# First norm of a diffusion backbone: its two modulation vectors on four column groups of TensorE, and the condition's silu later

## The chip, the cores and the metric

The kernel runs on one core of one Trainium2 chip. The metric is the device time of one execution in microseconds; lower is better. The kernel before took 3016.6 us (median of three runs, 3004.18 to 3018.82).

## The reference, cut to what matters

The network has two layers and works on 640 tokens: 512 latent tokens with a condition vector c and 128 context tokens with a learned vector c_ctx. Each layer is an FFN, a mixer and a second FFN, and each of these is preceded by a modulated norm. What the change touches is the first of them:

```python
mod = jax.nn.silu(cond) @ W['w_mod'][i] + W['b_mod'][i]
m = jnp.split(mod[:, None, :], N_MOD, axis=-1)
h = rms_norm(x, g_pre) * (1 + m[1]) + m[0]
f = (silu(h @ w1) * (h @ w3)) @ w2
x = x + 0.5 * m[2] * rms_norm(f, g_post)
```

Each layer has nine modulation vectors m[0] to m[8] of 1024 numbers for each of the two conditions. A vector is a product of 2 x 1024 by 1024 x 1024 in fp32.

## The kernel before

Tokens stand in columns and the 1024 features in eight tiles of 128 partitions. The tokens are split in two halves, of 384 and 256 columns. The order of instructions on each engine is made by a scheduler from the order of the text, from tile buffers and from its own estimates; it may bring an instruction forward whose inputs and buffers are free. Each engine, and each queue of loads (SP's for weights, ScalarE's for constants and the condition), works through its own order strictly.

The beginning (mods_first, lines 116 to 151). The condition is loaded transposed (1024 x 2, line 120), its silu taken on that small form, and silu_cond (line 124) loads the condition once more, spread over all partitions (1024 KB), and takes the silu of that on ScalarE and VectorE (lines 97 to 101). 24 products of ones run first on TensorE (line 127). Then, for k from 0 to 7, weights come as fp32 blocks of 128 x 1024. The scale m[1] is made on TensorE, in two products per k (line 134): the 128 x 2 condition is the stationary operand, 512 weight columns stream, and a 2 x 512 row builds up in PSUM over k. Of the shift m[0] the second half is made in the same way, one product per k. The first half of m[0] is made on VectorE (mods, lines 103 to 114, called at k < 4): the weight block comes transposed, and a multiply-and-sum over 1024 columns gives 128 numbers of one condition, twice per block. After k = 1 the input x is loaded. After k = 4 the text has x_rstd: squares on ScalarE (L209), sums on VectorE (L213), a small product (L176), a few VectorE steps, a diagonal dg (L190), and a product with ones (L192) that spreads the factor over all partitions. At the end the rows go from PSUM to SBUF on ScalarE (L145), are transposed in pieces of 128 columns (L148), and the bias is added (L149).

Then the norm itself (prenorm): x times the factor on VectorE (L255), scale and shift on GpSimd (L262) or ScalarE (L264), and a split in a high and a low part (L273, L274).

The first FFN. Its first stage has 22 hidden blocks and two token halves, 44 steps: blocks 0 to 2 of the first half, blocks 0 to 2 of the second, and from block 3 on both halves of each block in turn. A step has 48 products (L305 to L307) into two PSUM banks and ends in a tanh on ScalarE (L332) and two VectorE products (L333, L334). Weights of a block come as two raw tiles of 512 KB from SP's queue and are split on ScalarE (L299) and VectorE (L300). There are four raw tiles, shared by the FFN's weights and the modulation weights, and six buffers each for high and low parts; silu_cond takes its scratch tile from the low parts' ring. In run_ffn, after every fourth step (q = 3, 7, ...), mods makes the next modulation vector on VectorE: eight loads and 16 multiply-and-sum instructions (L111). In the first FFN seven vectors are made so, in the second nine; there the condition's buffer has been used by others in between, so silu_cond is called again, after step 10 (argument wait).

Of the kernel before, what the change touches and what calls it, by code (L numbers as in the profile page):

```python
# [9 lines left out]
F32 = mybir.dt.float32  # L10
# [4 lines left out]
ALU = mybir.AluOpType  # L15
PSUM = bass.MemoryType.PSUM

P = 128
# [20 lines left out]
class Net:  # L39
# [76 lines left out]
    def mods_first(self):  # L116

        nc, t = self.nc, self.t
        ct = self.fp.tile([P, KD, 2], F32, name="cond_t")
        nc.sync.dma_start(ct, t["cond_t"])  # L120
        th = self.fp.tile([P, KD, 2], F32, name="cond_s")
        nc.scalar.activation(th, ct, AF.Tanh, scale=0.5)
        nc.vector.scalar_tensor_tensor(ct, th, 1.0, ct, op0=ALU.add, op1=ALU.mult)
        self.silu_cond()
        rows = [[self.psum() for _ in range(2)] for _ in range(2)]
        for _ in range(24):
            nc.tensor.matmul(rows[0][0][:, 0:P], self.ones, self.ones, start=True, stop=True)
        for k in range(KD):
            for i in (1, 0):
                w = self.wp.tile([P, 1024], F32, tag="wl" if i else "wh", name=self.name("w"), bufs=self.nw)  # L130
                c0 = 0 if i else 512
                nc.sync.dma_start(w[:, c0:], t["w_mod_first"][i, k][:, c0:])
                for hf in range(1 - i, 2):
                    nc.tensor.matmul(rows[i][hf][0:2], ct[:, k], w[:, hf * 512:hf * 512 + 512], start=k == 0, stop=k == KD - 1)
            if k == 1:
                for j in range(KD):
                    nc.sync.dma_start(self.x[j], t["x"][:, j, :])
            if k < 4:
                self.mods(0, 0, (k,))
            if k == 4:  # L140
                rs = [self.x_rstd(hf) for hf in range(2)]
        for i in (1, 0):
            r = self.wp.tile([P, 1024], F32, tag="wl", name=self.name("row"), bufs=self.nw)[0:2]
            for hf in range(1 - i, 2):
                nc.scalar.activation(r[:, hf * 512:hf * 512 + 512], rows[i][hf][0:2], AF.Copy, scale=0.5)  # L145
            p, e0 = rows[i][1], 0 if i else 4
            for e in range(e0, KD):
                nc.tensor.transpose(p[:, 2 * e:2 * e + 2], r[:, e * P:(e + 1) * P], self.ident[0:2, 0:2])  # L148
            nc.vector.tensor_tensor(self.mall[:, i, e0:], p[:, 2 * e0:16].rearrange("p (e c) -> p e c", c=2),  # L149
                                    self.bmod[:, 0, i, e0:, None].to_broadcast([P, KD - e0, 2]), op=ALU.add)  # L150
        return [self.mall[:, i] for i in range(2)], rs

    def premod_scale(self, layer, sub, scale):
# [1123 lines left out]
def network(ctx, tc, t, outs):  # L1277
# [38 lines left out]
    with ExitStack() as c:  # L1316
        open_ffn(c)
        M[0][0:2], r = n.mods_first()
        gs, sh = gs_sh(0, 0)
        hs = [n.prenorm(hf, gs, sh, r=r[hf]) for hf in range(2)]  # L1320
        rk.consts()
        rk.dense_open(dram)
        hold = {}

        def after(hf, bank):
            a, b = HALF[hf]
            if hf == 0:
                hold["gs"] = gs_sh(0, 1)
            n.prenorm_to(hf, *hold["gs"], rk.dest, bank)
            for k in range(KD):  # L1330
                nc.sync.dma_start(xd[:, k, a:b], n.x[k][:, a:b])
            rk.shift(hf)
            if hf == 0:
                hold["first"] = rk.stream(1, 0, tag=0)

        run_ffn(0, hs, [(0, j) for j in range(2, 9)], 0, 0, after)
        rk.dense(hold["first"])
    with ExitStack() as c:
        sp = c.enter_context(tc.tile_pool(name="scan", bufs=1))
# [162 lines left out]
```

## Time and profile before

| | |
|---|---|
| median of three runs | 3016.6 us |
| the profiled execution's own time | 3012.7 us |
| its span, first to last instruction | 3010.9 us |
| mean granted clock of TensorE | 0.948 |
| TensorE busy | 2840.5 us, 94% |
| VectorE busy | 1804.1 us, 60% |
| ScalarE busy | 1070.7 us, 36% |
| GpSimd busy | 428.6 us, 14% |
| bytes moved | 384.63 MB, mean 128 GB/s |

The span runs from the first to the last instruction; the execution's own time is 1.8 us longer. PE is TensorE, DVE is VectorE, ACT is ScalarE, POOL is GpSimd; SPq and ACTq are the queues of loads of SyncE and ScalarE. A granted clock of 1.00 is 2.4 GHz, 0.50 is 1.2 GHz. An fp32 product shows as two passes, so 24 products are 48 rows. In brackets behind a row stands how long its engine was idle before it and what ended that.

### The profile page before, as it was taken

The numbers are of one execution on the slowest core, as the hardware profiler recorded it, in microseconds if no ns is written. First come the engines' busy times: TensorE is split into PE (matmuls) and PEld (weight loads), VectorE is DVE, ScalarE is ACT, GpSimd is POOL, SyncE is SP. The second block draws the span as 40 slices with busy tenths as digits, with TensorE's granted clock in tenths as the row PEclk, the third lists the DMA queues.
The fourth block names the chain that finished last, engine by engine and source line by source line (L and its number), as shares of the span: only waits on it lengthen the run. The fifth ranks groups of instructions, "written<-read, shape, count | busy, mean of one in ns | idle before, by whom it ended". The sixth has DMA issues, their size and how long they took to land.

```text
span 3010.9 us, 52286 instructions
## 1 busy us (share of the span) xinstructions
PE 2840.5 (94%) x20970; PEld 2539.9 (84%) x20970; DVE 1804.1 (60%) x3698; ACT 1070.7 (36%) x1916; POOL 428.6 (14%) x510
## 2 busy tenths in 40 slices
PE   8999999898899999999699999999999987999997
PEld 5999998585566666667599999999999986999997
DVE  7996328835566777664869993762332668323336
ACT  3112234234444554553431123541223445222233
POOL 2000033111001111101100004310002431000034
PEclk9999999998878998888899999999999998999999
DMA  6665233435433333124236664422223431222233
GB/s 248 206 221 179 81 126 138 162 119 164 125 91 110 119 120 114 50 66 160 88 127 216 225 220 152 140 93 77 71 81 109 139 124 67 99 71 78 91 119 126
DMA packets 167348, 384.63 MB, mean 128 GB/s; under 512 B 22721, under 2 KB 87873, under 8 KB 166849
## 3 DMA queue, kind: packets, MB, share of 16 engines
q1 hardware_dynamic: 165088, 378.22, 37.3%
q8 instruction: 164, 2.69, 0.4%
q10 hardware_dynamic: 2016, 3.07, 0.3%
q14 instruction: 80, 0.65, 0.1%
HBM read 353.24 MB, written 27.98 MB: 127 GB/s over the span
## 4 chain that ended last, share of the span: by engine, by line
PE 66%; DVE 17%; issue 6%; ACT 5%; DMA 4%; POOL 1%; SPq 0%; DVEq 0%; ACTq 0%; POOLq 0%
PE ps L306 15%; PE ps L305 15%; PE ps L307 15%; DVE cj L111 7%; PE px L699 4%; PE pg L843 2%; DVE wl L300 2%; PE pa L771 1%; DMA raw<-in_w_mod 1%; PE pc L981 1%; DVE t L213 1%; ACT gg L929 1%; PE ps L514 1%; PE px L667 1%; DMA mid<-xs 1%
## 5 line engine op out<-in xcount | busy, mean ns | idle before, releaser
L305 PE MATMUL ps<-hp,wh 128*128 128x384 f32 (+3 forms) x2968 | 920.8, 312 | 16.5 <-ACT hp L273 12.6
L306 PE MATMUL ps<-hp,wh 128*128 128x384 f32 (+3 forms) x2968 | 919.4, 310 | 4.5 <-DVE hp L495 2.1
L307 PE MATMUL ps<-hp,wl 128*128 128x384 f32 (+3 forms) x2968 | 915.9, 309 | 2.2 <-DVE wl L300 2.2
L300 DVE TENSOR_TENSOR wl<-raw,wh 128x1024 fp32r<-128x1024 f32 (+1 forms) x408 | 455.0, 1122 | 466.3 <-ACT wh L299 465.5
L299 ACT ACTIVATE wh<-raw 128x1024 fp32r<-128x1024 f32 (+1 forms) x408 | 388.9, 964 | 795.5 <-PE ps L306 675.2
L305 PEld LDWEIGHTS ps<-hp,wh 128*128 128x128 f32 x2968 | 561.1, 190 | 21.9 <-ACT hp L273 16.0
L306 PEld LDWEIGHTS ps<-hp,wh 128*128 128x128 f32 x2968 | 562.5, 190 | 7.4 <-DVE hp L495 2.3
L307 PEld LDWEIGHTS ps<-hp,wl 128*128 128x128 f32 x2968 | 560.5, 189 | 4.1 <-DVE wl L300 3.8
L359 POOL TENSOR_TENSOR gl<-t,gh 128x384 fp32r<-128x384 f32 (+1 forms) x176 | 237.1, 1348 | 1589.7 <-ACT gh L358 1559.7
L307 PE MATMUL ps<-gh,wl 128*128 128x384 f32 (+1 forms) x1408 | 438.6, 312 | 4.1 <-DVE wl L300 4.1
L306 PE MATMUL ps<-gl,wh 128*128 128x384 f32 (+1 forms) x1408 | 437.0, 311 | 3.8 <-POOL gl L359 3.8
L305 PE MATMUL ps<-gh,wh 128*128 128x384 f32 (+1 forms) x1408 | 437.0, 311 | 2.0 <-ACT gh L358 1.3
L111 DVE CUSTOM_DVE_ANT_0 cj<-raw,cj,bmod 128x1024 bf16<-128x1024 f32 x264 | 339.8, 1287 | 8.0 <-DMA raw<-in_w_mod 3.9
L306 PEld LDWEIGHTS ps<-gl,wh 128*128 128x128 f32 x1408 | 269.2, 191 | 5.5 <-POOL gl L359 4.8
L307 PEld LDWEIGHTS ps<-gh,wl 128*128 128x128 f32 x1408 | 269.4, 192 | 5.2 <-DVE wl L300 4.3
L305 PEld LDWEIGHTS ps<-gh,wh 128*128 128x128 f32 x1408 | 269.2, 191 | 4.0 <-ACT gh L358 1.5
L332 ACT ACTIVATE t<-ps 128x384 f32<-128x384 f32 (+1 forms) x176 | 75.7, 430 | 415.4 <-PE ps L307 415.4
L699 PE MATMUL px<-mid,pw 128*128 128x320 f32 x448 | 179.7, 514 | 7.8 <-DMA mid<-xs 5.5
L334 DVE TENSOR_TENSOR t<-t,ps 128x384 f32<-128x384 f32 (+1 forms) x176 | 85.4, 485 | 160.6 <-PE ps L307 160.3
L333 DVE SCALAR_TENSOR_TENSOR t<-t,ps 128x384 f32<-128x384 f32 (+1 forms) x176 | 85.1, 483 | 121.8 <-ACT t L332 121.8
L699 PEld LDWEIGHTS px<-mid,pw 128*128 128x128 f32 x448 | 82.1, 212 | 43.4 <-issue 14.5
L358 ACT ACTIVATE gh<-t 128x384 fp32r<-128x384 f32 (+1 forms) x176 | 79.9, 456 | 53.7 <-PE ps L307 28.8
(369 smaller groups left out, 3299.9 us busy)
## 6 DMA issues: line engine op xcount, KB each, us to landing
raw<-in_w SPq DMA_DIRECT2D x352, 512.0 KB, 3.2
raw<-in_w_mod SPq DMA_DIRECT2D x132, 512.0 KB, 4.1
mid<-xs SPq DMA_DIRECT2D x224, 160.0 KB, 2.3
pw<-in_w_rkv SPq DMA_DIRECT2D x28, 256.0 KB, 3.2
d<-po SPq DMA_DIRECT2D x28, 160.0 KB, 2.3
w<-in_w_mod_first SPq DMA_DIRECT2D x8, 512.0 KB, 7.7
raw<-in_w_rkv SPq DMA_DIRECT2D x8, 512.0 KB, 4.9
xs<-t SPq DMA_DIRECT2D x16, 191.0 KB, 1.9
```

Of the source, the lines that this page charges most:

```text
L111: nc.vector.tensor_tensor_reduce(self.junk, w, self.cond[:, i], 0.5, self.bmod[:, layer, idx, k:k + 1], ALU.mult, ALU.add, out[:, k, i:i + 1])
L299: nc.scalar.activation(h[:, c], w[:, c], AF.Copy)
L300: (eng or nc.vector).tensor_tensor(l[:, c], w[:, c], h[:, c], op=ALU.subtract)
L305: nc.tensor.matmul(out, wh, xh, start=start, stop=False)
L306: nc.tensor.matmul(out, wh, xl, start=False, stop=False)
L307: nc.tensor.matmul(out, wl, xh, start=False, stop=stop)
L332: nc.scalar.activation(gt, o[0], AF.Tanh, scale=0.5)
L333: nc.vector.scalar_tensor_tensor(gt, gt, 1.0, o[0], op0=ALU.add, op1=ALU.mult)
L334: nc.vector.tensor_tensor(gt, gt, o[1], op=ALU.mult)
L358: nc.scalar.activation(gh, g, AF.Copy)
L359: nc.gpsimd.tensor_tensor(gl, g, gh, op=ALU.subtract)
L699: nc.tensor.matmul(p[:, 0:320], w[k // 4][:, k % 4 * P:k % 4 * P + P], x, start=k == 0, stop=k == KD - 1)
```

## The change

All of m[0] and m[1] of the first norm are made on TensorE. For each k both weight blocks are loaded whole (2 x 512 KB), and four products follow, each 2 x 512, into four PSUM banks, where output c stands on partitions 32c and 32c + 1: each product uses another group of 32 columns of the array. The VectorE products of k < 4 and their loads are gone. The rows are copied out by ScalarE and VectorE, two each; 16 transposes of two rows follow, and four additions of the bias. silu_cond is no longer called in the beginning; the first FFN gets wait = 5: silu_cond is called after step 5, and the modulation vectors are made from step 7 on instead of step 3.

```diff
--- before.py
+++ after.py
@@ -121,33 +121,37 @@
         th = self.fp.tile([P, KD, 2], F32, name="cond_s")
         nc.scalar.activation(th, ct, AF.Tanh, scale=0.5)
         nc.vector.scalar_tensor_tensor(ct, th, 1.0, ct, op0=ALU.add, op1=ALU.mult)
-        self.silu_cond()
-        rows = [[self.psum() for _ in range(2)] for _ in range(2)]
+        rows = [self.psum() for _ in range(4)]
         for _ in range(24):
-            nc.tensor.matmul(rows[0][0][:, 0:P], self.ones, self.ones, start=True, stop=True)
+            nc.tensor.matmul(rows[0][:, 0:P], self.ones, self.ones, start=True, stop=True)
         for k in range(KD):
-            for i in (1, 0):
+            ws = []
+            for i in range(2):
                 w = self.wp.tile([P, 1024], F32, tag="wl" if i else "wh", name=self.name("w"), bufs=self.nw)
-                c0 = 0 if i else 512
-                nc.sync.dma_start(w[:, c0:], t["w_mod_first"][i, k][:, c0:])
-                for hf in range(1 - i, 2):
-                    nc.tensor.matmul(rows[i][hf][0:2], ct[:, k], w[:, hf * 512:hf * 512 + 512], start=k == 0, stop=k == KD - 1)
+                nc.sync.dma_start(w, t["w_mod_first"][i, k])
+                ws += [w[:, 0:512], w[:, 512:1024]]
+            for c in range(4):
+                nc.tensor.matmul(rows[c][32 * c:32 * c + 2], ct[:, k], ws[c], start=k == 0, stop=k == KD - 1)
             if k == 1:
                 for j in range(KD):
                     nc.sync.dma_start(self.x[j], t["x"][:, j, :])
-            if k < 4:
-                self.mods(0, 0, (k,))
             if k == 4:
                 rs = [self.x_rstd(hf) for hf in range(2)]
-        for i in (1, 0):
-            r = self.wp.tile([P, 1024], F32, tag="wl", name=self.name("row"), bufs=self.nw)[0:2]
-            for hf in range(1 - i, 2):
-                nc.scalar.activation(r[:, hf * 512:hf * 512 + 512], rows[i][hf][0:2], AF.Copy, scale=0.5)
-            p, e0 = rows[i][1], 0 if i else 4
-            for e in range(e0, KD):
-                nc.tensor.transpose(p[:, 2 * e:2 * e + 2], r[:, e * P:(e + 1) * P], self.ident[0:2, 0:2])
-            nc.vector.tensor_tensor(self.mall[:, i, e0:], p[:, 2 * e0:16].rearrange("p (e c) -> p e c", c=2),
-                                    self.bmod[:, 0, i, e0:, None].to_broadcast([P, KD - e0, 2]), op=ALU.add)
+        r = self.wp.tile([P, 1024], F32, tag="wl", name=self.name("row"), bufs=self.nw)
+        rw = [r[32 * c:32 * c + 2, 0:512] for c in range(4)]
+        for c in range(4):
+            if c % 2:
+                nc.scalar.activation(rw[c], rows[c][32 * c:32 * c + 2], AF.Copy, scale=0.5)
+            else:
+                nc.vector.tensor_scalar(rw[c], rows[c][32 * c:32 * c + 2], 0.5, None, op0=ALU.mult)
+        for e in range(4):
+            for c in range(4):
+                one = self.ident[32 * c:32 * c + 2, 32 * c:32 * c + 2]
+                nc.tensor.transpose(rows[c][:, 2 * e:2 * e + 2], rw[c][:, e * P:(e + 1) * P], one)
+        for c in range(4):
+            e = slice(c % 2 * 4, c % 2 * 4 + 4)
+            nc.vector.tensor_tensor(self.mall[:, c // 2, e], rows[c][:, 0:8].rearrange("p (e c) -> p e c", c=2),
+                                    self.bmod[:, 0, c // 2, e, None].to_broadcast([P, 4, 2]), op=ALU.add)
         return [self.mall[:, i] for i in range(2)], rs
 
     def premod_scale(self, layer, sub, scale):
@@ -1333,7 +1337,7 @@
             if hf == 0:
                 hold["first"] = rk.stream(1, 0, tag=0)
 
-        run_ffn(0, hs, [(0, j) for j in range(2, 9)], 0, 0, after)
+        run_ffn(0, hs, [(0, j) for j in range(2, 9)], 0, 0, after, 5)
         rk.dense(hold["first"])
     with ExitStack() as c:
         sp = c.enter_context(tc.tile_pool(name="scan", bufs=1))
```

## Rows read from the trace of the kernel before

**Rows 1.** The page: busy time of TensorE, and the chain by engine.
```profile
PE 2840.5 (94%) x20970; PEld 2539.9 (84%) x20970; DVE 1804.1 (60%) x3698; ACT 1070.7 (36%) x1916; POOL 428.6 (14%) x510
...
PE 66%; DVE 17%; issue 6%; ACT 5%; DMA 4%; POOL 1%; SPq 0%; DVEq 0%; ACTq 0%; POOLq 0%
```

**Rows 2.** Windows: stretch, length; busy of PE, PEld, DVE, ACT, POOL; clock; DMA share; GB/s.
```profile
15.00:20.00 5.00, 3.57 (x5) 0.59 (x6) 5.00 (x10) 3.88 (x12) 0.00 (x0) 0.50 1.04 403
...
40.00:45.00 5.00, 4.71 (x11) 0.77 (x9) 2.30 (x7) 1.97 (x4) 0.00 (x0) 1.00 0.01 2
...
50.00:55.00 5.00, 4.75 (x15) 4.76 (x16) 4.20 (x9) 4.86 (x11) 5.00 (x4) 0.50 0.41 140
```

**Rows 3.** Timeline, end of the beginning: start, us, engine, line, what, count [idle before].
```profile
37.91 0.70 PE L192 MATMUL ps<-dg,ones 128*128 128x256 f32 x2 [0.91 <-DVE dg L190]
...
38.54 6.17 PE L134 MATMUL ps<-w,cond_t 128*2 128x512 f32 x14
...
44.47 1.05 ACT L145 ACTIVATE row<-ps 2x512 f32<-2x512 f32 x2
...
45.09 0.90 PE L148 MATMUL ps<-ident,row 2*128 2x2 f32 x12 [0.38 <-ACT row L145]
...
46.45 16.26 POOL L262 TENSOR_SCALAR t<-t,gall,mall 128x384 f32<-128x384 f32 x16 [46.01 <-DVE gall L158]
...
50.25 1.33 PE L305 MATMUL ps<-hp,wh 128*128 128x384 f32 x3 [4.26 <-ACT hp L273]
```

**Rows 4.** By line, VectorE: ns min/median/max, first and last start.
```profile
L111 DVE CUSTOM_DVE_ANT_0 cj<-raw,cj,bmod x8: 1275/1277/1280, 15.6 to 34.0; 128x1024 bf16<-128x1024 f32 x8
...
L101 DVE SCALAR_TENSOR_TENSOR cj<-th,cj x4: 1217/1221/1225, 13.3 to 1548.4; 128x1024 f32<-128x1024 f32 x4
```

**Rows 5.** First FFN: ScalarE's timeline, TensorE's waits (60 to 200 us), SP's queue.
```profile
99.57 0.49 ACT L332 ACTIVATE t<-ps 128x384 f32<-128x384 f32 x1 [6.60 <-PE ps L307]
...
111.61 1.06 ACT L299 ACTIVATE wh<-raw 128x1024 fp32r<-128x1024 f32 x1 [4.67 <-DMA raw<-in_w]
...
276.17 0.49 ACT L332 ACTIVATE t<-ps 128x384 f32<-128x384 f32 x1 [3.24 <-PE ps L307]
...
PE ps L305 <- ACT wh L299: 3.4, 1, 3.4
...
108.38 7.54 SPq L294 DMA_DIRECT2D raw<-in_w  x4
```

**Rows 6.** Second FFN: timelines of ScalarE, its queue, and VectorE.
```profile
1406.90 0.33 ACTq L97 DMA_DIRECT2D cj<-in_cond  x1
...
1544.26 0.38 ACT L332 ACTIVATE t<-ps 128x256 f32<-128x256 f32 x1 [6.55 <-PE ps L307]
1544.54 1.05 ACT L100 ACTIVATE th<-cj 128x1024 f32<-128x1024 f32 x1
...
1551.27 0.49 ACT L332 ACTIVATE t<-ps 128x384 f32<-128x384 f32 x1 [3.32 <-PE ps L307]
...
1789.84 0.49 ACT L332 ACTIVATE t<-ps 128x384 f32<-128x384 f32 x1 [6.63 <-PE ps L307]
...
1548.43 1.22 DVE L101 SCALAR_TENSOR_TENSOR cj<-th,cj 128x1024 f32<-128x1024 f32 x1
```

**Rows 7.** Windows, first FFN: columns as in rows 2.
```profile
80.00:90.00 10.00, 10.00 (x88) 10.00 (x87) 9.89 (x17) 1.89 (x4) 1.43 (x1) 1.00 0.54 179
```

**Rows 8.** DMA issues to 60 us, then from 28 to 29: KB, us to landing.
```profile
w<-in_w_mod_first SPq DMA_DIRECT2D x8, 512.0 KB, 7.7
...
cj<-in_cond ACTq DMA_DIRECT2D x1, 1024.0 KB, 8.4
...
w<-in_w_mod_first SPq DMA_DIRECT2D x1, 256.0 KB, 7.8
```

**Rows 9.** Timeline of TensorE in the scan.
```profile
1411.45 0.22 PE L1011 MATMUL po<-gg,uv 128*64 128x64 f32 x1
1411.45 0.45 PE L1013 MATMUL po<-gg,uv 128*64 128x64 f32 x8
```

## The prediction

> **What bounds the kernel now.** I read the page's busy shares and its chain first. TensorE is busy 94% of the span and is named by 66% of the chain [rows 1], so time that is won before the first FFN product is kept only as long as TensorE finds its weights ready afterwards. The edit touches two stretches: the first 50 us, and the first FFN's first stage, where the other modulation vectors are made on VectorE.
>
> The beginning, by windows: from 15 to 20 us the DMA engines move 403 GB/s with a busy share of 1.04, and VectorE is busy all 5 us; by 40 us the transfers are over [rows 2]. What ends last is then read from the timeline. The second half's rstd product (L192) stands at 37.91 us and has waited for VectorE's dg; only behind it, in TensorE's own order, run the last 14 passes of the modulation products, from 38.54 to 44.71 us, on weights that are already there. ScalarE copies rows out to 45.52, the transposes end at 45.99, GpSimd starts the first normalised tile at 46.45 and TensorE the first FFN product at 50.25 us [rows 3]. So the beginning is held by VectorE: eight products of 1.28 us on the first vector (10.2 us) and two of 1.22 us for the silu [rows 4] lie between the sums of squares and dg.
>
> The FFN, by the tanh of each step, which marks the middle of a step on TensorE: the 24 steps between 99.57 and 276.17 us (12 hidden blocks of two halves) took 176.6 us. In the second FFN 34 steps between 1551.27 and 1789.84 us took 238.6 us, 14.03 us for a block of two halves [rows 5, 6]. At that pace the first FFN's 12 blocks would take 168.4 us, so it loses 8.2 us while VectorE makes modulation vectors (9.89 of 10 us busy [rows 7]). The largest single wait is 3.4 us for a weight split, because the weight's load was issued only at 108.38 us, behind eight modulation loads in SP's queue [rows 5].
>
> **The change, part by part.** (1) *Taken from VectorE*: 10.2 us for good, and 2.4 us of silu to a later place. The rstd of both halves is then made as soon as x has come, and L192 no longer holds the modulation products.
>
> (2) *Loads*. SP issued 8 x 512 + 8 x 256 KB of first-norm weights and 4 x 512 KB for the VectorE part, 8192 KB; it now issues 16 x 512 KB, the same bytes. The condition's 1024 KB is on ScalarE's queue. The last weights were issued just after 28 us and landed 7.8 us later, at about 35.9 us [rows 8]. If the condition's load really moves away, that becomes 1024 KB / 403 GB/s = 2.6 us earlier, 33.3 us. But in the second FFN the same load was issued at 1406.90 us, 138 us ahead of the tanh that needs it [rows 6]: the order puts a load where its buffer is free, not where the text stands. I take 35.9 us, and keep 33.3 for the range.
>
> (3) *Products*. 32 instead of 24 matmuls, of two passes each, 0.43 us a pass ((6.17 - 0.59) / 13 for the 14 in [rows 3]). One after another, four would take 3.44 us for each k, more than the 2.6 us in which their 1 MB comes in; fully side by side, 0.86 us. Four long streams on four column groups stand nowhere in the trace. The nearest rows are the scan's products on two groups of 64 columns: the second pass of one starts at 1411.45 us together with the first of the next, and eight passes take 0.45 us where each lasts 0.22 [rows 9]. Their starts are thus (0.45 - 0.22) / 7 = 0.033 us apart, against 0.053 for 64 columns streamed alone at the pace above (0.43 x 64 / 512). That is 1.6 times the serial pace, as if each matmul's second pass ran beside the next one's first. So I take 5 slots, 2.15 us, for each k: below the 2.6 us of the loads. TensorE keeps up, and after the last weight only its own two matmuls are left, three slots or 1.3 us.
>
> The Trainium skill, "TensorEngine Tiling (Array Packing)", Theoretical Speedup, gives up to 4 times for at most 32 columns; by that the four would take 0.86 us, the end would come 0.4 us sooner and the sum below would be 10.4 us. The scan's pairs, at 1.6 times, don't bear it out for a matmul of two passes.
>
> Products end at 35.9 + 0.2 + 1.3 = 37.4 us, against 44.7.
>
> (4) *Behind the products*. Two copies on each of ScalarE and VectorE, the last of them 0.6 us after the last product (two took 1.05 [rows 3]); 16 transposes of 0.075 us (12 took 0.90 [rows 3]) 1.2 us; four short additions and the scale, where two additions and the scale took 0.46 us from 45.99 to 46.45, 0.9 us; five handovers, estimated at 0.1 us. Sum 3.2 us, where 1.75 us stood before. GpSimd then starts at 40.6 us and the first FFN product comes 3.8 us later as now, at 44.4 us: 5.9 us earlier. With the load of the condition out of the way it is 8.5. If the groups ran one after another, products would fall behind the loads by 0.84 us for each of six k, 5 us, and only about 1 us would be left.
>
> (5) *The silu inside the FFN*. Its tanh needs a buffer of the ring that holds the low weight parts, so it waits for TensorE to finish with block 0: the first half of step 3. With S the start of the FFN that is S + 2.5 us (five us at a granted clock of 0.50, that is 1.2 GHz, as at 50 to 55 us [rows 2]) + three steps of the first half + half a step of the second. A block's 14 us, shared out by columns (384 and 256, an estimate), are 8.4 and 5.6, so that is S + 2.5 + 25.2 + 2.8 = S + 30.5. From the first tanh to the end of the last product took 5.1 us in the second FFN [rows 6], hence S + 35.6. ScalarE is held meanwhile, with the tanh of later steps behind it; eight PSUM banks, two a step, cover that. If the cover were gone it would cost up to those 5.1 us.
>
> (6) *Modulation vectors four steps later*. Each of the seven sets is now loaded between neighbouring weight blocks 4 to 16 (before: 3, 4, 6 ... 14). The weight of block 4 is queued on SP behind eight modulation loads, of which the fifth product pair must end: 10 x 1.28 = 12.8 us, plus two of 1.2 us for the split of block 3 and an estimated 3 us for the steps' own products. That gives S + 53.8. From its issue to ScalarE's split such a load took 111.61 - 108.38 = 3.2 us, the split 1.1 [rows 5], and VectorE's half of it should take the 1.2 us of a product of that size [rows 4]: S + 59.3. Block 4 is needed at S + 2.5 + 56 = S + 58.5. So it is just late; I put 1.5 us of wait there, where 0 and 5 are the ends. Later sets lose about what they lose now without that first wait. Of 8.2 us I expect 4 to be lost: 4 us gained, with -5 and +8 as ends.
>
> **Sum.** 5.9 + 4 = 10 us less. The profiled execution took 3012.7 us (span 3010.9), 3.9 us under the median of the three runs, so 3002.7 on its own footing and 3006.6 on the median's; I say 3006. Half a per cent, 15 us, is about what a measurement of this kernel can tell from no change, so this is a change in the right direction that mostly can't be told from none.
>
> **Rivals.** *More is won.* After its silu the second FFN makes nine vectors and loses almost nothing: 14.03 us a block [rows 6]. If the first FFN now does the same, all 8 us come back, and with the condition's load late the front gives 8.5. That is 16.5 us: 3000. For it: the same mechanism in the same kernel, with TensorE at 10 of 10 us. Against it: there the splits of two more blocks had been done before the first set.
>
> *The groups don't run side by side.* Then the edit doesn't do what it says, TensorE's products set the pace, the front gives 1 us and the FFN 4: 3011. Against it stand the scan's pairs; for it, that those streams are eight times shorter.
>
> *Slower: the silu comes too late.* If its tanh starts only where the text puts it, after step 5 at S + 2.5 + 42 = S + 44.5, everything in (6) comes 14 us later: block 4 is ready at S + 73.3, TensorE waits 14.8 us instead of 1.5, and after such a wait it starts at 1.2 GHz again, 2.5 us more. 10 - 15.8 is 6 us slower than before: 3022. The sign turns once that tanh starts later than about S + 39. Against it: in the second FFN the tanh started 0.28 us after that of a step's middle (1544.26), as its buffer came free [rows 6].
>
> **How the numbers follow.** Forecast 0.55, more won 0.25, serial groups 0.12, slower 0.08. The forecast's own range is 2998 to 3014, from the ends of (2) and (6); with the neighbours and the runs' own spread of 15 us, 2994 to 3019 holds eight times in ten. Faster by over 0.5%: over half of the second case (its time lies just beyond the bound) and a quarter of the first, 0.27. Slower by over 0.5%: a third of the last case, 0.03. Within: 0.70.
>
> **What would show it.** The first FFN product near 44 us (42 to 45); no row of VectorE's modulation product before it; L134 with 64 passes whose starts, in a group of eight, are spread over about 2 us; the last weight landing near 36 us. The tanh of the silu at S + 30; TensorE's wait for a weight split around S + 58 of under 5 us; the middle of step 30 (276.17 before) near 266. It would be wrong if the passes stand 0.43 us apart throughout, if the FFN starts before 41 us, or if TensorE waits over 10 us behind the silu.

## The result, and the profile after

The new kernel took 2993.58 us (median of 9 runs, 2989.17 to 3002.74), the kernel before 3018.95 us in the runs beside it (9 runs, 3004.18 to 3034.62). The ratio is 0.9917 [0.9898, 0.9937]: 25 us less, where 10 were forecast. The profiled execution took 2997.18 us, its span 2995.4. On the page TensorE's busy time is what it was [rows 1], over a shorter span, and its share of the chain rose from 66 to 75%:

```profile
PE 2836.9 (95%) x20990; PEld 2539.7 (85%) x20990; DVE 1796.1 (60%) x3686; ACT 1071.0 (36%) x1915; POOL 423.3 (14%) x510
...
PE 75%; DVE 12%; ACT 4%; issue 4%; DMA 3%; POOL 1%; SPq 0%; DVEq 0%; ACTq 0%; POOLq 0%
```

**The beginning.** Lines after L151 stand four further down than before (the norm's GpSimd row is L266, the FFN's products L309 to L311). The timeline of the new kernel, against [rows 3]:

```profile
3.24 0.39 ACTq L97 DMA_DIRECT2D cj<-in_cond  x1
...
35.60 0.28 PE L150 MATMUL ps<-ident,row 2*128 2x2 f32 x2 [0.71 <-ACT row L144]
...
35.81 1.03 PE L134 MATMUL ps<-w,cond_t 128*2 128x512 f32 x4
...
37.56 0.46 PE L150 MATMUL ps<-ident,row 2*128 2x2 f32 x8 [0.37 <-ACT row L144]
...
38.61 13.17 POOL L266 TENSOR_SCALAR t<-t,gall,mall 128x384 f32<-128x384 f32 x16 [38.17 <-DVE gall L162]
...
41.33 0.69 PE L309 MATMUL ps<-hp,wh 128*128 128x384 f32 x1 [3.31 <-ACT hp L277]
```

Read it from the bottom: the first FFN product stands at 41.33 us instead of 50.25, 8.9 us earlier. GpSimd starts at 38.61, 7.8 us earlier, and the last product of the first vectors ends at 36.84 (35.81 + 1.03) instead of 44.71. The top row shows the condition's 1024 KB still loaded at 3.24 us, although the text calls silu_cond only inside the FFN, after step 5: its buffer was free. Two transposes at 35.60 run ahead of the last four passes, since two rows were finished by then; six more follow right behind those passes (36.77 us).

**The first stage of the first FFN.** In the windows (columns as in [rows 2]) TensorE is full from 60 us on. In the first 20 us of the stage it is not: there it waits for the second half's norm tiles, while GpSimd is still busy with them.

```profile
40.00:50.00 10.00, 8.14 (x32) 7.10 (x33) 6.12 (x12) 7.82 (x18) 10.00 (x13) 0.72 0.15 52
50.00:60.00 10.00, 8.91 (x51) 7.89 (x51) 8.18 (x12) 8.41 (x13) 1.78 (x4) 1.00 0.41 116
60.00:70.00 10.00, 10.00 (x60) 10.00 (x59) 7.51 (x10) 3.33 (x6) 1.56 (x2) 1.00 0.45 161
```

The waits of TensorE, from 30 to 400 us of the new kernel (waiting for; us in total, times, longest) hold no row for the high weight part any more:

```profile
PE ps L309 <- ACT hp L277: 4.0, 4, 3.3
PE ps L150 <- ACT row L144: 1.1, 2, 0.7
PE ps L310 <- DVE hp L278: 0.6, 2, 0.3
PE ps L311 <- DVE wl L304: 0.3, 1, 0.3
```

In the kernel before, from 60 to 400 us, the high part cost 3.8 us (3.4 of them in one wait [rows 5]) and the low part 2.2:

```profile
PE ps L305 <- ACT wh L299: 3.8, 2, 3.4
PE ps L307 <- DVE wl L300: 2.2, 5, 0.5
```

The silu on ScalarE's timeline: the second tanh there is that of block 0's *second* half (256 columns), and behind it, with one weight split between, comes the silu's first instruction, at 58.95 us, 17.6 us after the start of the FFN. The last row is the tanh of the stage's last step on the first half, which stood at 359.97 us before.

```profile
53.52 0.49 ACT L336 ACTIVATE t<-ps 128x384 f32<-128x384 f32 x1
56.75 0.37 ACT L336 ACTIVATE t<-ps 128x256 f32<-128x256 f32 x1
58.95 1.05 ACT L100 ACTIVATE th<-cj 128x1024 f32<-128x1024 f32 x1
62.38 1.05 ACT L100 ACTIVATE th<-cj 128x1024 f32<-128x1024 f32 x1
...
344.92 0.49 ACT L336 ACTIVATE t<-ps 128x384 f32<-128x384 f32 x1 [3.24 <-PE ps L311]
```

On TensorE the second half's first 24 products of block 0 stand right behind the first half's first 24, ahead of everything else of the first half. The next two rows are the first of these products and the first product behind them:

```profile
47.73 0.28 PE L309 MATMUL ps<-hp,wh 128*128 128x256 f32 x1
...
53.78 0.34 PE L309 MATMUL ps<-hp,wh 128*128 128x384 f32 x1
```

They took 6.05 us, since they had to wait for the second half's norm. Without gaps they would take 2.8: half of a step of the second half, whose share of the 14.03 us of a block [rows 6] is 5.6 by columns, an estimate.

The first GpSimd row of the FFN's second stage is the milestone used from here on. First the kernel before, then the new one:

```profile
375.31 1.64 POOL L359 TENSOR_TENSOR gl<-t,gh 128x384 fp32r<-128x384 f32 x1 [290.88 <-ACT gh L358]
```

```profile
360.26 1.64 POOL L363 TENSOR_TENSOR gl<-t,gh 128x384 fp32r<-128x384 f32 x1 [280.07 <-ACT gh L362]
```

So 15.05 us are won by the end of the stage: 8.9 in front of it, and 6.1 in the stage itself, which went from 325.1 us (375.31 - 50.25) to 318.9 (360.26 - 41.33).

### The profile page after: what moved, and what is told of

The parts are those of the page before. It is cut to its first block, busy times and chain, and to the rows that moved or that the text cites. A ratio compares the mean times of both kernels' runs of the same rounds, so it can differ in the third digit from the quotient of the medians.

```text
span 2995.4 us, 52305 instructions
## 1 busy us (share of the span) xinstructions
PE 2836.9 (95%) x20990; PEld 2539.7 (85%) x20990; DVE 1796.1 (60%) x3686; ACT 1071.0 (36%) x1915; POOL 423.3 (14%) x510
## 4 chain that ended last, share of the span: by engine, by line
PE 75%; DVE 12%; ACT 4%; issue 4%; DMA 3%; POOL 1%; SPq 0%; DVEq 0%; ACTq 0%; POOLq 0%
PE ps L310 17%; PE ps L309 17%; PE ps L311 17%; PE px L703 5%; DVE cj L111 4%; PE pg L847 2%; PE pa L775 2%; PE pc L985 1%; DVE wl L304 1%; PE px L671 1%; PE ps L518 1%; ACT gg L933 1%; DVE t L217 1%; PE pc L974 1%; PE pc L993 1%
## 5 line engine op out<-in xcount | busy, mean ns | idle before, releaser
L309 PE MATMUL ps<-hp,wh 128*128 128x384 f32 (+3 forms) x2968 | 920.2, 312 | 12.3 <-ACT hp L277 12.3
L311 PE MATMUL ps<-hp,wl 128*128 128x384 f32 (+3 forms) x2968 | 915.4, 309 | 0.3 <-DVE wl L304 0.3
L309 PEld LDWEIGHTS ps<-hp,wh 128*128 128x128 f32 x2968 | 560.6, 189 | 17.2 <-ACT hp L277 15.8
L311 PEld LDWEIGHTS ps<-hp,wl 128*128 128x128 f32 x2968 | 560.2, 189 | 0.7 <-DVE wl L304 0.5
L311 PE MATMUL ps<-gh,wl 128*128 128x384 f32 (+1 forms) x1408 | 436.9, 311 | 4.1 <-DVE wl L304 4.1
L309 PE MATMUL ps<-gh,wh 128*128 128x384 f32 (+1 forms) x1408 | 435.1, 310 | 2.0 <-ACT gh L362 1.3
L111 DVE CUSTOM_DVE_ANT_0 cj<-raw,cj,bmod 128x1024 bf16<-128x1024 f32 x256 | 329.6, 1288 | 8.3 <-DMA raw<-in_w_mod 3.9
L311 PEld LDWEIGHTS ps<-gh,wl 128*128 128x128 f32 x1408 | 267.8, 190 | 5.2 <-DVE wl L304 4.3
L309 PEld LDWEIGHTS ps<-gh,wh 128*128 128x128 f32 x1408 | 267.5, 190 | 3.8 <-ACT gh L362 1.7
```

The lines of the kernel that those rows point to most:

```text
L111: nc.vector.tensor_tensor_reduce(self.junk, w, self.cond[:, i], 0.5, self.bmod[:, layer, idx, k:k + 1], ALU.mult, ALU.add, out[:, k, i:i + 1])
L309: nc.tensor.matmul(out, wh, xh, start=start, stop=False)
L311: nc.tensor.matmul(out, wl, xh, start=False, stop=stop)
```

## The experiments

The theory after this reading: two gains that need each other. The products on TensorE give some 9 us in front of the FFN; the vectors made four steps later give the stage back its lost time. The first rival: the front alone does it. The second: the silu's new place does it. A third question was whether the column groups really run side by side.

All results in one table. "Start" is the first FFN product, "stage 2" the milestone above, "stage" their difference, "waits" what TensorE waited for weight splits between 60 and 400 us; all in us. A ratio is to the kernel before in the same runs.

| kernel | median | ratio [95%] | start | stage 2 | stage | waits |
|---|---|---|---|---|---|---|
| before | 3018.95 | 1 | 50.25 | 375.31 | 325.1 | 6.0 |
| new | 2993.58 | 0.9917 [0.9898, 0.9937] | 41.33 | 360.26 | 318.9 | 0 |
| products_only | 3013.48 | 0.9984 [0.9961, 1.0007] | 41.76 | 375.10 | 333.3 | 10.4 |
| late_vectors_early_silu | 2995.13 | 0.9928 [0.9902, 0.9954] | 41.94 | 360.86 | 318.9 | 0 |
| before_late_vectors | 3001.22 | 0.9958 [0.9936, 0.9979] | 50.02 | 365.63 | 315.6 | 0 |
| one_group | 3013.96 | 0.9994 [0.9976, 1.0012] | 52.96 | 380.07 | 327.1 | 7.6 |
| half_vectors | 3004.20 | 0.9952 [0.9932, 0.9972] | 49.45 | 365.23 | 315.8 | 0.3 |
| front_without_vector_engine | 3013.62 | one run | 47.95 | 380.53 | 332.6 | 11.5 |
| condition_on_sp | 2991.30 | 0.9910 [0.9883, 0.9938] | 39.99 | 358.94 | 319.0 | 0 |
| vectors_from_11 | 2997.26 | 0.9927 [0.9899, 0.9955] | 41.96 | 361.37 | 319.4 | 0 |
| condition_on_sp_vector_norm | 3009.98 | 0.9973 [0.9952, 0.9995] | 37.81 | 374.55 | 336.7 | 6.5 |

### The two parts, each alone

*products_only*: the new beginning, with the silu and the vectors where they were before.

```diff
+        self.silu_cond()
         rows = [self.psum() for _ in range(4)]
...
-        run_ffn(0, hs, [(0, j) for j in range(2, 9)], 0, 0, after, 5)
+        run_ffn(0, hs, [(0, j) for j in range(2, 9)], 0, 0, after)
```

> The new kernel with the condition's silu back in the beginning and the modulation vectors from step 3 on, as before: only the first norm's products are on the four groups. If the beginning and the first FFN's first stage gain separately, the first FFN product starts near 41.5 to 43 us (41.3 in the new kernel, 50.25 before), the stage still loses some 8 us to late weight splits, and the whole gains 9 us against before (ratio 0.997). If the later vectors are worth nothing and all the gain is from the beginning, it gains as much as the new kernel, 25 us (ratio 0.992).

Measured: 0.9984 [0.9961, 1.0007]. The FFN starts 8.5 us earlier than before, and stage 2 at 375.10, 0.2 us earlier. The whole gain in front was handed back inside the stage; the waits of TensorE from 60 to 400 us tell at which point:

```profile
PE ps L310 <- ACT wh L304: 7.1, 4, 4.3
PE ps L312 <- DVE wl L305: 3.3, 3, 1.6
```

*late_vectors_early_silu*: the new kernel with the silu back in the beginning, the vectors still from step 7.

```diff
+        self.silu_cond()
         rows = [self.psum() for _ in range(4)]
...
-            if q == wait and wait:
+            if q == wait and wait and i:
                 n.silu_cond()
```

> The new kernel with the silu back in the beginning, but the vectors still from step 7 on. If it is the later start of the vectors that removes the waits of the stage, TensorE waits under 1 us for weight splits between 60 and 340 us and the time is that of the new kernel within 3 us. If moving the silu matters (its VectorE products delay the norm, its scratch tile delays a weight split), it differs from the new kernel by 3 us or more, and the first FFN product starts 2 us later.

Measured: 0.9928 [0.9902, 0.9954], stage 2 at 360.86. Against the place where the new kernel's silu came to stand (58.95 us), the early place is worth nothing that can be measured, and the stage has the same length (318.9 us). What a later silu goes with is seen in one_group below.

*before_late_vectors*: the old beginning, the vectors from step 7.

```diff
-            if q == wait and wait:
+            if q == wait and wait and i:
                 n.silu_cond()
...
-        run_ffn(0, hs, [(0, j) for j in range(2, 9)], 0, 0, after)
+        run_ffn(0, hs, [(0, j) for j in range(2, 9)], 0, 0, after, 5)
```

> The kernel before with one number changed: the vectors of the first FFN start at step 7 instead of step 3, the silu stays in the beginning. The first FFN product stays at 50 us. If the later start alone removes the waits, the stage between the middles of steps 6 and 30 takes 168 us instead of 176.6 and the whole gains 6 to 9 us (ratio 0.997 to 0.998). If the waits vanish only because VectorE has less to do in the beginning, the gain is under 2 us.

Measured: 0.9958 [0.9936, 0.9979], a start as before (50.02) and no wait for a split:

```profile
365.63 1.64 POOL L359 TENSOR_TENSOR gl<-t,gh 128x384 fp32r<-128x384 f32 x1 [282.23 <-ACT gh L358]
```

The stage takes 315.6 us. So the later vectors are worth 9.5 us by themselves, the products nothing by themselves, and both together 15. The stage of the new kernel is 3.3 us longer than this one, about what the 24 products at 47.73 us lost there (6.05 us instead of 2.8): TensorE now comes before the second half's norm is ready.

The 6.0 us of split waits before are not the whole of the 9.5. After its long wait (it ended at 112.72 us) TensorE's granted clock was 0.56 in the mean of the next 3 us and 0.83 in that of ten, which is another 1.7 us of full clock; before_late_vectors has 1.00 and 69 products in the same window:

```profile
110.00:120.00 10.00, 7.08 (x32) 6.79 (x33) 9.34 (x17) 3.89 (x5) 0.00 (x0) 0.83 0.65 231
```

In products_only it is 0.82 and 0.84 from 100 to 120 us, 3.4 us on top of its 10.4 us of waits. The remaining 2 us of the 9.5 were not traced.

### What the vectors cost the stage

*half_vectors*: the kernel before, each vector of the first FFN made for one condition only.

```diff
-                M[a][b] = n.mods(a, b)
+                M[a][b] = n.mods(a, b, n=2 if i else 1)
```

> The kernel before, with the first FFN's modulation vectors made for one of the two conditions only (the other half is set to zero): half of VectorE's 112 products of that stage, at the old place (from step 3 on) and with the same loads. If the stage is bound by the end of VectorE's products (262.1 us before, 260.1 with the first norm's products moved alone, whatever the start of the FFN), then with half of them TensorE waits for no weight split, the first low part of the second stage comes at 365 to 367 us instead of 375.3, and the time falls by 10 to 16 us, as with the later vectors. If the later vectors gain for another reason (their loads, the silu, the order of the rest), it falls by under 4 us.

Measured: 0.9952 [0.9932, 0.9972], and 0.3 us of waits. With 56 products on VectorE instead of 112 the stage takes 315.8 us, as with all of them made later. The loads are the same in number, so it is the time that VectorE takes over them, not the traffic of eight loads a vector, that makes the splits late: its own, and ScalarE's by way of the raw buffers, which the next loads wait for (from 60 to 280 us SP's queue waited 97.9 us for these products in the kernel before, 57.1 us here).

*vectors_from_11*: the new kernel with the vectors still four steps later, and the silu with them, after step 9.

```diff
-        run_ffn(0, hs, [(0, j) for j in range(2, 9)], 0, 0, after, 5)
+        run_ffn(0, hs, [(0, j) for j in range(2, 9)], 0, 0, after, 9)
```

> The new kernel with the silu after step 9 and the vectors from step 11 on, another four steps later. If the later vectors gain because the last of them no longer stands ahead of a weight block that TensorE is waiting for, nothing is left to gain, as TensorE waits for 0.3 us of splits in the whole stage: the same time within 3 us. If later is better in itself, the time falls by another 5 us or more.

Measured: 0.9927 [0.9899, 0.9955], stage 2 at 361.37. Once no split is late, later is worth nothing.

Why four steps are enough is in when VectorE ends. The last modulation product, in the kernel before, in products_only and in the new kernel:

```profile
262.07 1.28 DVE L111 CUSTOM_DVE_ANT_0 cj<-raw,cj,bmod 128x1024 bf16<-128x1024 f32 x1
```

```profile
260.11 1.28 DVE L111 CUSTOM_DVE_ANT_0 cj<-raw,cj,bmod 128x1024 bf16<-128x1024 f32 x1
```

```profile
267.73 1.28 DVE L111 CUSTOM_DVE_ANT_0 cj<-raw,cj,bmod 128x1024 bf16<-128x1024 f32 x1
```

The 112 products take 145 us of VectorE in each, and only their first start moved, from 53.61 to 61.61 and 64.21. VectorE is busy nearly all the time while it works through them (29.45 of the 30 us from 70 to 100 us before, 29.68 in products_only), and so the end does not follow an earlier start of the FFN. Each set has to be finished before the split of a weight block behind it in the order, the last set before block 14. In the new kernel that is block 16, two blocks of 14.03 us later [rows 6]. Counted from the start of the FFN, the deadline moved by 28 us and the last product by 14.6, from 211.8 to 226.4. In products_only it moved too, to 218.4, with the old deadline.

### The beginning

*one_group*: the new kernel with all four outputs on the same group of columns.

```diff
-                nc.tensor.matmul(rows[c][32 * c:32 * c + 2], ct[:, k], ws[c], start=k == 0, stop=k == KD - 1)
+                nc.tensor.matmul(rows[c][0:2], ct[:, k], ws[c], start=k == 0, stop=k == KD - 1)
```

> The new kernel with all four products of a k on the first 32 columns of the array instead of on four groups; nothing else of the computation is changed. If the four groups are what makes TensorE keep up with the loads, the 64 passes stand 0.43 us apart or more, the products end 4 to 6 us later (41 to 43 us instead of 36.8), and the first FFN product starts at 45 to 48 us: 5 us of the gain are lost. If the loads set the pace anyway, it starts within 1.5 us of 41.3 and the time is that of the new kernel within 3 us.

Measured: 0.9994 [0.9976, 1.0012]. Its timeline of TensorE:

```profile
22.62 12.65 PE L134 MATMUL ps<-w,cond_t 128*2 128x512 f32 x24
...
37.63 9.60 PE L134 MATMUL ps<-w,cond_t 128*2 128x512 f32 x22
...
52.96 1.01 PE L309 MATMUL ps<-hp,wh 128*128 128x384 f32 x2 [4.66 <-ACT hp L277]
```

22 passes take 9.60 us, 0.43 each, one behind the other, and products end at 47.23 us. The same stretch of products_only, with its four groups:

```profile
31.58 3.62 PE L135 MATMUL ps<-w,cond_t 128*2 128x512 f32 x32
```

32 passes in 3.62 us, four k of eight passes: 0.9 us for each k, two slots of 0.43. The four groups run fully side by side. The weights came in as before (402 GB/s from 28 to 35 us), so 10.4 of the 11.6 us between the two starts (52.96 against 41.33) are those of the serial products (47.23 against 36.84). The rest lies in the tail behind them, 5.73 us against 4.49.

This kernel also shows what a later silu goes with. TensorE takes the first half's three steps in a row here, and the second half's first product comes at 80.26 us:

```profile
84.39 1.05 ACT L100 ACTIVATE th<-cj 128x1024 f32<-128x1024 f32 x1
```

That is 31.4 us after the start of the FFN, not 17.6. The vectors start at 86.95 us, the last product 234.7 us after the start, not 226.4, and the stage loses 7.6 us to split waits although its vectors begin at step 7: 2.2 of them on block 4, the rest later. before_late_vectors, with the same order of steps, a start 2.9 us earlier and the silu in the beginning, loses none, and its stage is 11.5 us shorter.

*front_without_vector_engine*: the kernel before, with the VectorE products of the beginning left out and their loads kept.

```diff
             if k < 4:
-                self.mods(0, 0, (k,))
+                nc.sync.dma_start(self.raw([P, 1024]), t["w_mod"][0, k])
...
+        nc.vector.memset(self.mall[:, 0, 0:4], 0.0)
```

> The kernel before without the VectorE products of the first vector's first half (that half of the shift is set to zero; its weights are still loaded, so the bytes are the same). If those products hold the beginning, the rstd is ready earlier, the modulation products end with their loads at 37 to 39 us instead of 44.7, and the first FFN product starts at 42 to 45 us instead of 50.25, without any column groups. If TensorE's own order or the loads hold it, it stays above 48 us. The whole is then like the first kernel of the last call: no more than 5 us faster, since the vectors still start at step 3.

Measured in one run: a start at 47.95 us, 2.3 earlier than before and well short of the new kernel. The timeline shows what takes VectorE's place:

```profile
30.43 13.04 PE L134 MATMUL ps<-w,cond_t 128*2 128x512 f32 x30
```

30 passes in a row, 13.04 us. VectorE was not alone in holding the beginning: behind it stood TensorE's serial passes. To take 9 us away both had to go, and the four groups are the part that does it.

*condition_on_sp*: the new kernel with the condition's 1024 KB on SP's queue, where it comes behind the weights.

```diff
-        nc.scalar.dma_start(self.cond, t["cond"][None, :, :].to_broadcast([P, 2, 1024]))
+        nc.sync.dma_start(self.cond, t["cond"][None, :, :].to_broadcast([P, 2, 1024]))
```

> The new kernel with the condition's 1024 KB load on SP's queue, where it stands behind the first norm's weights and five FFN weights, instead of on ScalarE's at 3.2 us. If the loads set the end of the beginning, the last weight lands 2.6 us earlier and the first FFN product starts near 38.7 us instead of 41.3, and the time falls by up to 2.6 us (ratio to before 0.991). If rstd or the tail holds it, it starts within 0.7 us of 41.3. The silu may come later; if that delays the vectors, TensorE waits for splits in the stage, and the time is 3 us longer or more.

Measured: 0.9910 [0.9883, 0.9938], start at 39.99, stage 2 at 358.94. On SP's timeline the load is issued at 38.92 us instead of 3.24:

```profile
38.92 0.43 SPq L97 DMA_DIRECT2D cj<-in_cond  x1
```

The start moves by 1.3 us, half of the 2.6 us that the prediction gave this load, and it is kept. By its median it is the fastest of all, but its interval holds the new kernel's ratio.

*condition_on_sp_vector_norm*: the same, with the first norm's GpSimd pieces on VectorE.

```diff
-                    nc.gpsimd.tensor_scalar(o, i_, gs[:, k, cd:cd + 1], sh[:, k, cd:cd + 1], op0=ALU.mult, op1=ALU.add)
+                    (nc.vector if first else nc.gpsimd).tensor_scalar(o, i_, gs[:, k, cd:cd + 1], sh[:, k, cd:cd + 1], op0=ALU.mult, op1=ALU.add)
```

> The new kernel with the condition's load on SP's queue, as in the last call, and in the first norm the pieces of scale and shift that GpSimd made (16, 13.2 us) on VectorE, which is idle for a third of that time. If the first FFN starts as soon as the norm's first tiles are there and then starves for the second half's tiles (TensorE busy 17 of 20 us between 40 and 60), it starts 1 us earlier than the 40.0 us of the last call and loses 2 us less: the second stage starts near 356 us instead of 358.9, the ratio to before is 0.990. If VectorE then becomes late with the low parts, nothing is gained: 0.991 or more.

Measured: 0.9973 [0.9952, 0.9995]. The earliest start of all (37.81) and the longest stage (336.7): the splits are late once more. The two rows count from 30 us on, 9.2 us in all; 2.7 of them lie ahead of 60 us.

```profile
PE ps L311 <- DVE wl L304: 7.2, 5, 2.7
...
PE ps L309 <- ACT wh L303: 2.0, 2, 1.3
```

Here too the silu is late, at 78.76 us (57.91 in condition_on_sp), 41.0 us after the start, and the last modulation product starts at 282.00 instead of 264.94 us. How much of the loss is VectorE's extra work in the norm and how much the later silu was not taken apart.

### Is the rest of the gain real?

Stage 2 starts 15 us earlier, yet the medians differ by 25. Both kernels were run again, with a kernel before that is unchanged as its own control, and with one that differs only in four products of ones fewer at the start.

```diff
-        for _ in range(24):
+        for _ in range(20):
             nc.tensor.matmul(rows[0][0][:, 0:P], self.ones, self.ones, start=True, stop=True)
```

> The kernel before, unchanged, for a second profile. The two profiled executions shown so far differ by 15.5 us, the medians by 24. If the rest lies in the first FFN's first stage (its waits vary from run to run), the second stage starts at 380 us or later instead of 375.3. If it lies behind that stage, where both kernels have the same order of instructions, the second stage starts within 2 us of 375.3 and the time from there to the end is more than the 2637 us of the first look, about 2642.

> As the second look: start of the second stage at 375 us and about 2642 us from there if the scatter lies behind the stage, 380 us or later if it lies in it.

> The new kernel, unchanged, for a second profile. In the first look the second stage started at 360.3 us and the rest took 2637 us. If the stage without waits is steady, it starts within 2 us of that again, and what differs between runs lies behind it: about 2633 us, if the median of 2993.6 is typical.

> The kernel before, unchanged, timed against itself: what the measurement itself scatters. The ratio should be 1.000 with an interval of some 0.002 to either side. If unchanged code gives a ratio of 0.997 or less, the 10 us that the profiles don't show are scatter of the measurement.

> The kernel before with 20 instead of 24 products of ones at the very start of TensorE, the rest in the same order. The first FFN should start within 1 us of 50, the second stage within 1 us of 375. If any edit that moves the scan against the TensorE clock takes about 7 us off (as in the other variants, whose medians fell by 4 to 9 us more than the start of their second stage), the ratio is 0.997 to 0.998. If it is a property of the later vectors, the ratio is 1.000.

> The new kernel, unchanged, timed once more. If its whole gain is 24 us, the ratio is 0.992 again. If 14 us of the second stage's earlier start are all that the edit gives and the rest was the scan's scatter in one measurement, it is 0.995.

| kernel | time | ratio [95%] | stage 2 | scan | stage 2 to the end |
|---|---|---|---|---|---|
| before, first profile | 3018.95 | 1 | 375.3 | 733.7 | 2635.6 |
| before_second_look | 3015.88, one run | | 374.5 | 736.5 | 2639.6 |
| before_third_look | 3022.52, one run | | 374.4 | 739.7 | 2646.3 |
| before_null | 3020.65 | 1.0000 [0.9980, 1.0019] | 379.7 | 740.1 | 2642.7 |
| fewer_warmups | 3026.74 | 1.0014 [0.9996, 1.0031] | 380.3 | 740.1 | 2646.0 |
| new, first profile | 2993.58 | 0.9917 [0.9898, 0.9937] | 360.3 | 740.5 | 2635.1 |
| new_second_look | 3008.21, one run | | 361.0 | 746.7 | 2644.4 |
| new_again | 2992.66 | 0.9916 [0.9887, 0.9945] | 360.6 | 747.0 | 2650.6 |

Times and ratios are those of all runs of a row, the last three columns those of its one profiled execution (the scan from its first projection to its last chain product). Two things follow. The ratio of the new kernel came out the same twice, and the control at 1.000, so the 25 us stand. fewer_warmups, which shifts the start of TensorE and removes nothing behind it, came out at 1.0014: an edit as such takes nothing off. And the profiles place 13 to 19 us of them at the end of the first stage: 360.3 to 361.0 in three executions of the new kernel, 374.4 to 379.7 in four of the one before. The kernel before scatters there because its split waits do. The profile of before_null has 9.1 us of them where the first had 6.0:

```profile
PE ps L305 <- ACT wh L299: 7.1, 5, 4.4
PE ps L307 <- DVE wl L300: 2.0, 4, 0.5
```

What is left of the difference, some 6 to 12 us, lies behind the first stage by subtraction. The profiles of these two kernels do not show it: the rest of the program took 2635 to 2646 us in the kernel before and 2635 to 2651 in the new one, with the same instructions in it in the same order. But the profiled executions of the new kernel in the second table (2997.18, 3008.21 and 3012.99 us) all lie above its medians in the tables. Their granted clock from 670 to 1420 us, about the scan, was 0.85, against 0.87 to 0.88 in the four of the kernel before. Two kernels with the same program behind the first stage were caught at the speed of the new kernel's medians: late_vectors_early_silu (2989.85 us) and condition_on_sp (2991.30). There the clock of that stretch was 0.88 and 0.89 and the rest took 2626.9 and 2630.6 us, 5 to 19 less than in the kernel before. So what is left goes with the clock of the scan, as far as these profiles tell. Whether the new beginning brings a higher clock about more often is open: over nine profiles with the new beginning the rest took 2626.9 to 2650.6 us, over eight with the old one 2631.3 to 2651.0.

## Why the prediction was wrong, step by step

The direction and both places of the gain were right; the forecast was 10 us where 25 came, a little outside the range's lower end, and "faster by over 0.5%" had been given 0.27. The step whose mechanism failed is (5), the time of the silu, and with it (6), which is worked out from it. Of the 15 us that the sum lacks, the steps below account for 5: 0.6 in (3), 2.5 in (4), 2.1 in (6). The other 10 lie behind the first stage, by subtraction. The sum puts that part at nothing without a reason; it goes with the clock of the scan, as far as the profiles tell, and its cause is open.

**(1) VectorE and (2) the loads** held. Its rows of the modulation product before the FFN are gone; the condition's load stayed early, as step 2 took it, and the last weight's products started at 35.81 us, against 35.9 for its landing.

**(3) The products** ended at 36.84 us, not 37.4. The step put five slots on each k, from the scan's pairs of 64 columns; the rows of products_only and one_group show two, 0.9 us against 3.44 one after another. All first passes of the four groups start together, and then all second passes (in products_only four within 0.02 us at 31.58 us, the next four at 32.01); the scan's pairs hide that, with 0.22 us long streams whose starts 0.033 us apart may have had another limit. The Trainium skill, "TensorEngine Tiling (Array Packing)", Theoretical Speedup, with its up to 4 times for at most 32 columns, was set aside there. The rows agree with it: 3.8 times (3.44 against 0.9). The five slots, together with the estimated landing, cost the forecast no more than 0.6 us at the end, since the loads set the pace either way. That the groups matter at all is one_group's answer: the rival "groups don't run side by side" was priced at 3011 us, and the kernel that makes it true took 3013.96. That the two are close is luck: the rival had 1 us won in front and 4 in the stage, and one_group starts the FFN 2.7 us later than before and has a stage 2.0 us longer.

**(4) The tail** was put at 3.2 us and took 1.77 (36.84 to 38.61). The step let all copies and 16 transposes follow the last product. Half of the copies and two of the transposes ran ahead of the last passes, and six more transposes followed while the other rows were copied: a row was finished as soon as its own group was. From GpSimd's start to the first FFN product it took 2.72 us, not 3.8. TensorE waits there for ScalarE's high part, and that for GpSimd's first tile. The tile took 2.78 us before, beside two weight splits on VectorE, and 1.70 now, beside one; first the kernel before, then the new one:

```profile
46.45 2.78 POOL L262 TENSOR_SCALAR t<-t,gall,mall 128x384 f32<-128x384 f32 x1 [46.01 <-DVE gall L158]
46.49 2.36 DVE L300 TENSOR_TENSOR wl<-raw,wh 128x1024 fp32r<-128x1024 f32 x2 [0.15 <-ACT wh L299]
```

```profile
38.61 1.70 POOL L266 TENSOR_SCALAR t<-t,gall,mall 128x384 f32<-128x384 f32 x1 [38.17 <-DVE gall L162]
38.61 1.24 DVE L304 TENSOR_TENSOR wl<-raw,wh 128x1024 fp32r<-128x1024 f32 x1
```

Together with step 3 the front gave 8.9 us, not 5.9.

**(5) The silu** came 13 us earlier than the step said: at S + 17.6 instead of S + 30.5. The step counted three steps of the first half ahead of the second half's first step. The scheduler put the second half's first 24 products at 47.73 us, right behind the first half's first 24; they are the last to read the first low part, and so its buffer of the ring could come free. one_group, where the order is the one that the step counted, has the silu at S + 31.4. Nothing waits for ScalarE meanwhile, as the step had it.

**(6) The vectors.** "Of 8.2 us I expect 4 to be lost": no wait for a high part is left, 0.3 us for a low part, and the stage is 6.1 us shorter (9.5 with the old beginning). The step saw block 4's split as just late because it began from the silu at S + 30.5. With the silu at S + 17.6 the vectors start at S + 22.9 (64.21 us), and that lateness is gone. The reckoning itself held where its premise did: in one_group block 4 cost 2.2 us of waits, where the step put 1.5. And it took later sets to "lose about what they lose now". In one_group they lose 5.4 us; in the new kernel the two more blocks of time that each has are enough.

**The rivals.** "More is won", given 0.25, is what happened. It expected all 8 us back and 8.5 in front, 16.5 in sum; 15.05 are measured at the end of the stage, 6.1 and 8.9. The agreement in front is luck: its 8.5 needed the condition's load out of the way, and that load stayed at 3.24 us; what came is the shorter end of (3) and (4). Its objection (the second FFN had two more blocks split before its first set) was not needed. "Slower" needed the silu's tanh after S + 39, and it came at S + 17.6. Beyond this rival lies the part of the 25 us that the profiles of the two kernels do not place.

One reading of the first part was only half right. "The beginning is held by VectorE" is true of the order in [rows 3], but front_without_vector_engine gains 2.3 us: TensorE's serial passes stood next, and the prediction never asked what they would do if VectorE alone were taken away. Nor do the two products of the silu lie between the sums of squares and dg: they ran from 13.33 to 15.69 us, the first sum at 16.82.

## What to carry to other kernels

An earlier start of a stage is worth nothing if another engine works through a fixed lump in it whose end sets the later waits: products_only started 8.5 us earlier and ended 0.2 us earlier. Look at when that engine ends and which consumer it must beat, and move the lump behind a later deadline; here that alone was worth 9.5 us. Then check what releases the lump: the same later deadline was missed in one_group, where the silu ahead of the vectors came 14 us later against the start of the FFN. Where a thin product leaves most of the array's columns idle, put its outputs on different groups of columns, and then ask what limits next: here it was the loads.

## What the runs showed of the hardware

Four fp32 products with two output rows each, on four groups of 32 columns, took the time of one: 32 passes in 3.62 us, where one group needed 0.43 us for each pass, both at a granted clock of 1.00.

A tile of 128 x 384 took GpSimd 1.70 us beside one weight split on VectorE and 2.78 us beside two.

The same scan took 729.7 us in the profile of late_vectors_early_silu and 747.0 in that of new_again, with the same instructions in the same order. The windows from 670 to 1400 us, first the one and then the other, differ in the granted clock (0.88 and 0.85) and in how many matmuls got done in them (7070 and 6849):

```profile
670.00:1400.00 730.00, 701.32 (x7070) 474.99 (x7068) 458.98 (x1224) 350.03 (x668) 79.51 (x162) 0.88 0.36 109
```

```profile
670.00:1400.00 730.00, 701.75 (x6849) 471.43 (x6848) 458.13 (x1218) 347.30 (x659) 78.15 (x160) 0.85 0.35 106
```

A scatter of 17 us in one stage is more than the gain that this change has in another; a single profile cannot place a gain of this size by its total, only by the milestones of the stage that it touches.
